# Attention scores of two token tiles at a time, with the lower-part products on half the rows of the array

## The chip, the core and the metric

The kernel runs on one core of a Trainium2 chip. The metric is the device time of one execution, in microseconds (us). The engines that matter here are PE (TensorE, the matrix engine; its weight loads are listed apart as PEld), DVE (VectorE), ACT (ScalarE), POOL (GpSimd) and SP, which issues most of the DMAs.

## The reference

The kernel computes one decoder layer for 1024 tokens of width 1024. Two token mixers run side by side: an attention with three branches (compressed blocks, selected blocks, a sliding window of 512) and an attention over a latent with an index that selects 256 keys for each query. Both have 8 heads. Their outputs are projected, gated, merged and normalized, and a mixture of 32 experts with a second normalization follows. The change touches only the logits of the attention:

```python
logits = jnp.einsum('tghd,gtkd->ghtk', q, k_g) * scale + bias          # selected blocks
logits = jnp.einsum('tghd,kgd->ghtk', q, kw) * scale + rel_a[...]       # window
logits = jnp.einsum('tghd,cgd->ghtc', q, k_cmp) * scale + rel_a[...]    # compressed blocks
logits = jnp.einsum('thr,tkr->htk', q_lat, c_g) * HEAD_DIM ** -0.5 + bias  # latent
```

A head has 64 values per query and key.

## The kernel before

All matrix products are made from numbers that are split into a higher part and a lower part (`split`, lines 58 to 60: ACT copies the higher part in the fp32r type, DVE subtracts it). For the scores a head's queries lie in one tile `q` of 128 partitions: `load_query` (L475 to L479) puts the higher part of the 64 values on partitions 0 to 63 and the lower part on partitions 64 to 127, with two DMAs of 256 KB, issued by SP. The keys' higher part lies in `kh` and the lower part in `kl`; each is held twice, on both halves of the partitions. One matmul of `q` with `kh` therefore gives (higher + lower query) times higher key, and one of `q` with `kl` adds the same with the lower key, into the same PSUM tile.

The tokens are cut into 8 tiles `i` of 128. `nsa_head` (L548) makes a head of the first mixer: for each half `gq` (four token tiles) and each `part` (0: selected blocks, 1: window and compressed blocks) it goes over the four tiles. A tile's score row has 128 x (i + 1) columns in part 0, at most 640 in part 1, and is cut into chunks of 512 columns. Every chunk is one matmul with `kh` (L573) and one with `kl` (L574). In part 1 a product of 64 columns with the compressed keys follows (L580 with `kch`, L581 with `kcl`). `dsa_head` (L631) does the same for the second mixer (L651 with `kh`, L652 with `kl`), and for tiles from 2 on a third matmul adds the selection as a mask (L654). Each score row has a PSUM tile `s` of two banks, and there are two of these (`ps.open("psa", s=2, pt=3, pv=1)`).

`softmax_part` (L481) then adds the bias on DVE (L482) and takes the exponential on ACT (L484); POOL scales the rows (L465). `values` (L523) transposes the probabilities on PE (L490, into the PSUM tiles `pt`), splits them (L59, L60), and multiplies them with the values (L545 and L546, into `pv`). Heads of the two mixers alternate (`ORDER`). The order of the instructions of each engine is made by a scheduler at build time that simulates the engines: it keeps the program's order as a priority and fills gaps with what is ready, so scores of one head stand between transposes and value products of another.

The only matmuls before that don't use all 128 rows of the array are those of `bias_tables` (L293, L294): nine pairs on 33 rows, between full-row matmuls of the projections (L204) and of the compressed blocks (L393).

Of the kernel before, what the change touches and what calls it, by code (L numbers as in the profile page):

```python
# [9 lines left out]
F32 = mybir.dt.float32  # L10
# [8 lines left out]
P = 128  # L19
T = 1024  # L20
# [24 lines left out]
def layer_kernel(ctx: ExitStack, tc: tile.TileContext, A, out, dbg=None):  # L45
    nc = tc.nc
    V, S, G, PE = nc.vector, nc.scalar, nc.gpsimd, nc.tensor
# [7 lines left out]
    def f(ap):  # L55
        return ap.bitcast(F32)
# [10 lines left out]
    class Psum:  # L67
# [7 lines left out]
        def tile(self, shape, dt, name):  # L75
            return self.pool.tile(shape, dt, name=name, bufs=self.bufs[name])

    ps = Psum()
# [3 lines left out]
    qkd = {n: (dr.tile([P, T], F32, name=f"h_{n}"), dr.tile([P, T], F32, name=f"l_{n}"))  # L82
           for n in TILES[3:15] if n not in ("kc", "vc")}
# [18 lines left out]
    ident_b = cst.tile([P, P], BF, name="ident_b")  # L102
# [10 lines left out]
    kch = att.tile([P, 2, 64], F32R, name="kch")  # L113
    kcl = att.tile([P, 2, 64], F32R, name="kcl")
# [6 lines left out]
    OFF = {}  # L121
# [5 lines left out]
    selm = att.tile([P, NIDX], BF, name="selm")  # L127
# [9 lines left out]
    with tc.tile_pool(name="cr", bufs=1, side="right") as cr, tc.tile_pool(name="cr2", bufs=2, side="right") as cr2:  # L137
        big = [ps.tile([P, T], F32, name="s") for _ in range(3)]
        acc = [b[:, c] for b in big for c in HALF] + [ps.tile([P, 512], F32, name=n) for n in ("pt", "pv")]
        for k in range(KD):  # L140
# [7 lines left out]
            for i in range(NT):  # L148
                ts = slice(i * P, (i + 1) * P)
# [78 lines left out]
    with tc.tile_pool(name="ix", bufs=1, side="right") as ix, tc.tile_pool(name="ixl", bufs=2, side="right") as ixl:  # L228
        qs = []
        for n in ("qi0", "qi1"):  # L230
            z = project(n)
            for j in range(2):
                t = ix.tile([P, T], F32R, name=f"qs{len(qs)}")
                a, b = slice(j * 64, j * 64 + 64), slice(64 - j * 64, 128 - j * 64)
# [7 lines left out]
        for g in range(2):  # L242
            t = ps.tile([P, 512], F32, name="pt")
# [180 lines left out]
    with tc.tile_pool(name="cp", bufs=1, side="right") as cp, tc.tile_pool(name="bt", bufs=1, side="right") as bt:  # L424
        bias = bias_tables(bt)
        for n in ("kc", "vc"):
            j = TILES.index(n)
            compress_in(n, cp)
            c = compress(n, cp)
# [28 lines left out]
    pwp = pws.enter_context(tc.tile_pool(name="pwp", bufs=1))  # L458
# [3 lines left out]
    aw1 = aw.enter_context(tc.tile_pool(name="aw1", bufs=3, side="right"))  # L462
# [10 lines left out]
        return t[:, 0], t[:, 1]  # L473

    def load_query(t, n, j):  # L475
        r = slice(j * 64, j * 64 + 64)
        for x in range(2):
            nc.sync.dma_start(f(t[x * 64:x * 64 + 64]), qkd[n][x][r])
        return t  # L479

    def softmax_part(s, m, p, st, j):  # L481
        V.tensor_tensor_reduce(p, s, m, scale=1.0, scalar=3.0e38, op0=ALU.add, op1=ALU.min,  # L482
                               accum_out=st[:, 0, j:j + 1])
        S.activation(p, p, AF.Exp, bias=st[:, 0, j:j + 1], scale=-1.0, accum_out=st[:, 1, j:j + 1])  # L484
# [16 lines left out]
    mc = aw0.tile([P, 8, 120], F32, name="mc")  # L501
# [47 lines left out]
    def nsa_head(h, kv, fin):  # L549
        g = h // 4  # L550
        ksh, ksl, kwh, kwl = kv
        if h % 2 == 0:
            pair["q"], pair["m"], pair["w"] = slot(2, [P, 2, T], F32R), slot(3, [P, 2, T]), slot(4, [P, 2, T])
        q, m, mw = (pair[x][:, h % 2] for x in "qmw")
        load_query(q, f"qa{h // 2}", h % 2)
        nc.sync.dma_start(m, toeplitz(b_d[h], WD, T))
        nc.sync.dma_start(mw[:, 0:640], toeplitz(bw_d[h], WW, 640))
        for gq in range(2):
            o = ps.tile([P, 512], F32, name="pv")
            I4 = range(4 * gq, 4 * gq + 4)  # L560
            todo = []
            for part in range(2):
                st = aw1.tile([P, 2, 8], F32, name="st", bufs=3)
                PR, PC, PS = {}, {}, {}
                for i in I4:
                    ts = slice(i * P, (i + 1) * P)
                    k0 = 0 if part == 0 else max(0, i - 4)
                    n = P * (i + 1 - k0)
                    kh, kl = (ksh, ksl) if part == 0 else (kwh, kwl)
                    s = ps.tile([P, T], F32, name="s")  # L570
                    for c in range(0, n, 512):
                        e = min(n, c + 512)
                        PE.matmul(s[:, c:e], q[:, ts], kh[:, k0 * P + c:k0 * P + e], start=True, stop=False)  # L573
                        PE.matmul(s[:, c:e], q[:, ts], kl[:, k0 * P + c:k0 * P + e], start=False, stop=True)  # L574
                    j = i % 4
                    if part == 0:
                        PR[i] = aw1.tile([P, T], F32, name="pb", bufs=8)[:, :n]
                        softmax_part(s[:, :n], m[:, T - n:T], PR[i], st, j)
                    else:
                        PE.matmul(s[:, 640:704], q[:, ts], kch[:, g], start=True, stop=False)  # L580
                        PE.matmul(s[:, 640:704], q[:, ts], kcl[:, g], start=False, stop=True)  # L581
                        pb = pwp.tile([P, 704], F32, name="pw", bufs=6)
                        PR[i], PC[i], PS[i] = pb[:, :n], pb[:, n:n + 64], pb[:, n - 64:n + 64]
                        softmax_part(s[:, :n], mw[:, 640 - n:640], PR[i], st, j)
                        softmax_part(s[:, 640:704], mc[:, h, 56 - 8 * i:120 - 8 * i], PC[i], st, 4 + j)
                w = 4 + 4 * part
                V.tensor_scalar(st[:, 1, :w], st[:, 1, :w], 1e-30, None, op0=ALU.max)
                V.reciprocal(st[:, 1, :w], st[:, 1, :w])
                V.tensor_tensor(st[:, 1, 0:4], st[:, 1, 0:4], sig[:, 4 * gq:4 * gq + 4, 3 * h + 1 + part], op=ALU.mult)
                if part:  # L590
                    V.tensor_tensor(st[:, 1, 4:8], st[:, 1, 4:8], sig[:, 4 * gq:4 * gq + 4, 3 * h], op=ALU.mult)
                for i in I4:
                    scale_rows(PR[i], st[:, 1, i % 4:i % 4 + 1])
                    if part:
                        scale_rows(PC[i], st[:, 1, 4 + i % 4:5 + i % 4])
                for k in range(4 * gq + 4):
                    ii = [i for i in I4 if i >= k and (part == 0 or i - 4 <= k)]
                    k0 = [0 if part == 0 else max(0, i - 4) for i in range(NT)]
                    todo.append((vv[:, k, 2 * part + g],
                                 [PR[i][:, (k - k0[i]) * P:(k - k0[i] + 1) * P] for i in ii], ii[0]))  # L600
                if part:
                    todo.append((vcc[:, g], [PS[i] for i in I4], 4 * gq))
                values(o, todo, gq, part == 0, part == 1)
                todo = []
            finish("a", h, gq, o, fin)
# [24 lines left out]
    def dsa_head(h, vb, fin):  # L630
        m = aw2.tile([P, T], F32, name="m")  # L631
        nc.sync.dma_start(m, toeplitz(b_d[8 + h], WD, T))
        q = load_query(aw2.tile([P, T], F32R, name="q"), f"qb{h // 2}", h % 2)
        s = ps.tile([P, T], F32, name="s")
        for w, c in ((ukh, cth), (ukh, ctl), (ukl, cth)):
            for x in HALF:
                PE.matmul(s[:, x], w[:, h], c[:, x], start=(w is ukh and c is cth), stop=(w is ukl))
        kh = aw2.tile([P, T], F32R, name="kbh", bufs=1)
        kl = aw2.tile([P, T], F32R, name="kbl", bufs=1)
        split(kh, kl, s)  # L640
        for gq in range(2):
            I4 = range(4 * gq, 4 * gq + 4)
            PR = {}
            st = aw1.tile([P, 2, 4], F32, name="st", bufs=3)
            for i in I4:
                ts = slice(i * P, (i + 1) * P)
                n = P * (i + 1)
                s = ps.tile([P, T], F32, name="s")
                for c in range(0, n, 512):
                    e = min(n, c + 512)  # L650
                    PE.matmul(s[:, c:e], q[:, ts], kh[:, c:e], start=True, stop=False)  # L651
                    PE.matmul(s[:, c:e], q[:, ts], kl[:, c:e], start=False, stop=i < 2)  # L652
                    if i >= 2:
                        PE.matmul(s[:, c:e], ident_b, selm[:, OFF[i] + c:OFF[i] + e], start=False, stop=True)  # L654
                PR[i] = aw1.tile([P, T], F32, name="pb", bufs=8)[:, :n]
                softmax_part(s[:, :n], m[:, T - n:T], PR[i], st, i % 4)
            V.tensor_scalar(st[:, 1], st[:, 1], 1e-30, None, op0=ALU.max)
            V.reciprocal(st[:, 1], st[:, 1])
            for i in I4:
                x = st[:, 1, i % 4:i % 4 + 1]  # L660
                if (i % 2 and h >= 6):
                    V.tensor_scalar(PR[i], PR[i], x, None, op0=ALU.mult)
                else:
                    scale_rows(PR[i], x)
            o = ps.tile([P, 512], F32, name="pv")
            todo = []
            for k in range(4 * gq + 4):
                ii = [i for i in I4 if i >= k]
                todo.append((vb[:, k, h % 2], [PR[i][:, k * P:(k + 1) * P] for i in ii], ii[0]))
            values(o, todo, gq, True, True)  # L670
            finish("b", h, gq, o, fin)
# [148 lines left out]
    with tc.tile_pool(name="wo", bufs=1, side="right") as wo, tc.tile_pool(name="wo2", bufs=2, side="right") as wo2:  # L820
# [147 lines left out]
        for i in range(NT):  # L968
            ts = slice(i * P, (i + 1) * P)
            s = ps.tile([P, T], F32, name="s")  # L970
            last = i == NT - 1
# [343 lines left out]
```

## Time and profile before

| | us |
|---|---|
| median of three runs | 1434.45 (1433.2 to 1434.85) |
| the profiled execution | 1431.84 |
| its span, first to last instruction | 1430.1 |
| PE busy | 1331.9 (93%) |
| DVE busy | 1114.9 (78%) |
| ACT busy | 764.4 (53%) |
| POOL busy | 460.3 (32%) |

The attention, which the change touches, lies between 435 and 835 us. A matmul's busy time in the profile holds its way through the array too, and matmuls overlap, so the pace of the PE is read from the distance between starts and not from durations.

### The profile page before, as it was taken

What the parts mean: (1) busy time and instruction counts of PE and PEld (TensorE: products, weight loads), DVE (VectorE), ACT (ScalarE), POOL (GpSimd) and SP (SyncE); (2) the same over time, 40 slices, a digit from 0 to 9 for tenths busy, and PEclk for the clock granted to TensorE, in tenths of its full rate; (3) what the DMA queues carried; (4) which work ended last, traced back from release to release, by engine and by line L of the source; (5) the groups of instructions that cost most, each with busy time, mean ns of one, the idle gap of its engine ahead of it and who ended that gap; (6) DMA issues with size and microseconds to landing.
All of it is one profiled execution on the core that took longest, in us unless ns stands there. A gap on an engine that the chain in (4) does not pass through costs nothing. (4 is left out here: it accounts for less than half of the span.)

```text
span 1430.1 us, 20066 instructions
## 1 busy us (share of the span) xinstructions
PE 1331.9 (93%) x6779; PEld 1100.2 (77%) x6795; DVE 1114.9 (78%) x2273; ACT 764.4 (53%) x1378; POOL 460.3 (32%) x463
## 2 busy tenths in 40 slices
PE   8999999999999999999999999999969999998960
PEld 7878888878887787888878778888757778776640
DVE  5323699889997787888889965655869999998856
ACT  4323323221116788888879731211238888886744
POOL 1112323222223335453444100001334454443326
PEclk9999999999998999999999999999969999999985
DMA  6023334498333232732521264664659999999936
GB/s 234 16 74 133 111 116 149 152 279 285 138 106 112 67 107 90 195 105 82 152 74 38 97 264 160 253 237 154 230 186 329 344 325 317 317 329 329 320 74 235
DMA packets 69477, 261.36 MB, mean 183 GB/s; under 512 B 15092, under 2 KB 16974, under 8 KB 57085
## 3 DMA queue, kind: packets, MB, share of 16 engines
q1 hardware_dynamic: 59644, 243.24, 49.3%
q0 software_dynamic: 9728, 16.82, 5.1%
q8 instruction: 54, 0.88, 0.3%
q14 instruction: 51, 0.41, 0.1%
HBM read 219.19 MB, written 70.70 MB: 203 GB/s over the span
## 5 line engine op out<-in xcount | busy, mean ns | idle before, releaser
L1089 PE MATMUL pt<-slot,slot 128*128 128x512 f32 x768 | 199.9, 407 | 10.3 <-DVE slot L1077 4.9
L1077 DVE TENSOR_TENSOR slot<-slot,slot 128x1024 fp32r<-128x1024 f32 x160 | 191.3, 1219 | 15.8 <-ACT slot L1076 11.7
L1076 ACT CAST slot<-slot 128x1024 fp32r<-128x1024 f32 x160 | 165.8, 1048 | 36.9 <-PE pt L1089 25.9
L1089 PEld LDWEIGHTS pt<-slot,slot 128*128 128x128 f32 x768 | 142.1, 192 | 49.7 <-DVE slot L1077 8.9
L186 POOL TENSOR_TENSOR wl<-wr,wh 128x1024 fp32r<-128x1024 f32 x39 | 94.9, 2434 | 264.5 <-ACT wh L185 256.0
L324 DVE TENSOR_SCALAR_CACHE_REDUCE jk<-idx,cand 128x384 bf16<-128x384 f32 (+1 forms) x186 | 164.4, 942 | 1.2
L60 DVE TENSOR_TENSOR ptl<-pt,pth 128x512 fp32r<-128x512 f32 (+1 forms) x240 | 148.5, 638 | 18.5 <-ACT pth L59 17.5
L204 PE MATMUL s<-xh,wh 128*128 128x512 f32 x496 | 154.9, 393 | 2.4 <-DVE wi L168 1.4
L204 PE MATMUL s<-xh,wl 128*128 128x512 f32 x496 | 154.5, 391 | 0.0
L204 PE MATMUL s<-xl,wh 128*128 128x512 f32 x496 | 154.4, 391 | 0.0
L59 ACT CAST pth<-pt 128x512 fp32r<-128x512 f32 (+1 forms) x240 | 127.8, 548 | 45.4 <-PE pt L490 38.6
L465 POOL TENSOR_SCALAR pb<-pb,st 128x128 f32<-128x128 f32 (+3 forms) x120 | 91.7, 783 | 183.1 <-ACT pth L59 55.5
L185 ACT CAST wh<-wr 128x1024 fp32r<-128x1024 f32 x39 | 41.0, 1051 | 190.9 <-PE s L204 92.2
L1117 POOL DMA_INDIRECT acc_d<-wr,tkv x32 | 76.8, 2400 | 138.7 <-DVE wr L1116 132.5
L204 PEld LDWEIGHTS s<-xh,wh 128*128 128x128 f32 x496 | 92.5, 188 | 22.9 <-issue 2.6
L204 PEld LDWEIGHTS s<-xl,wh 128*128 128x128 f32 x496 | 93.6, 189 | 19.5
L204 PEld LDWEIGHTS s<-xh,wl 128*128 128x128 f32 x496 | 93.4, 189 | 19.3
L484 ACT ACTIVATE pb<-pb,st 128x128 f32<-128x128 f32 (+7 forms) x128 | 99.6, 779 | 15.5 <-DVE st L482 14.4
L1112 PE MATMUL s<-slot,hT 128*128 128x512 f32 x384 | 100.7, 408 | 2.0 <-DVE hT L60 1.5
L982 PE MATMUL s<-slot,slot 128*128 128x512 f32 x384 | 93.5, 398 | 0.0
L1112 PEld LDWEIGHTS s<-slot,hT 128*128 128x128 f32 x384 | 70.6, 191 | 26.8 <-DVE hT L60 11.2
L490 PE MATMUL pt<-ident,pb 128*128 128x128 f32 x576 | 90.5, 276 | 0.7 <-DVE ptl L60 0.4
(340 smaller groups left out, 2918.8 us busy)
## 6 DMA issues: line engine op xcount, KB each, us to landing
slot<-in_w_ex_dram SPq DMA_DIRECT2D x80, 1024.0 KB
wr<-in_w_tt_dram SPq DMA_DIRECT2D x31, 512.0 KB
ring<-in_w_ex_dram SPq DMA_DIRECT2D x11, 1024.0 KB
b_d<-r_d SPq DMA_DIRECT2D x16, 576.0 KB
xw<-in_xw_dram SPq DMA_DIRECT2D x8, 718.0 KB
last<-in_w_ex_dram SPq DMA_DIRECT2D x5, 1024.0 KB
z_ga<-sh SPq DMA_DIRECT2D x8, 512.0 KB
slot<-b_d SPq DMA_DIRECT2D x8, 512.0 KB
```

Of the source, the lines that this page charges most:

```text
L59: S.copy(h, src)
L60: V.tensor_tensor(l, src, f(h), op=ALU.subtract)
L186: G.tensor_tensor(wl, wr, f(wh), op=ALU.subtract)
L204: PE.matmul(z[:, c], w[:, k * P:(k + 1) * P], xx[:, k, c], start=(k == 0 and w is wh and xx is xh), stop=(k == KD - 1 and w is wl))
L324: V.tensor_scalar(jk[:, :n], idx[:, OFF[i]:OFF[i] + n], t, None, op0=op, op1=ALU.add, accum_out=cnt[:, i - 2:i - 1])
L465: G.tensor_scalar(ap, ap, s, 1.0, op0=ALU.mult, op1=ALU.mult)
L484: S.activation(p, p, AF.Exp, bias=st[:, 0, j:j + 1], scale=-1.0, accum_out=st[:, 1, j:j + 1])
L982: mm = PE.matmul(s[:, HALF[c]], MS[i][:, a, k], WO[k][:, b, HALF[c]], start=(k == 0 and x == 0), stop=(k == KD - 1 and x == 2)).ins
L1076: S.copy(w[:, 0], self.w[k2 // 4][:, k2 % 4 // 2])
L1077: d = V.tensor_tensor(w[:, 1], self.w[k2 // 4][:, k2 % 4 // 2], f(w[:, 0]), op=ALU.subtract).ins
L1089: PE.matmul(self.a, self.xt[:, a, k * P:(k + 1) * P], w[:, b, (k - k2) * 512:(k - k2 + 1) * 512], start=(k == 0 and x == 0), stop=(k == KD ...
L1112: PE.matmul(s[:, c], self.hT[:, a, k * P:(k + 1) * P], w[:, b, c], start=(k == 0 and x == 0), stop=(k == 1 and x == 2))
```

## The change

`load_query` keeps the old stacking for even token tiles and turns it round for odd ones (the lower part on partitions 0 to 63, the higher part on 64 to 127). It issues four DMAs for a head instead of two, each of half the size with pieces of 128 tokens. A new helper `scores` takes two token tiles at a time. For each chunk it issues the full-row products with `kh` of both tiles, then the products with `kl`, each on 64 rows only: rows 0 to 63 for the even tile and 64 to 127 for the odd one. These rows hold the query's higher part, so the product of the two lower parts is no longer formed. The products with `kl` are tied behind the last one with `kh` of the chunk. In `dsa_head` the masks of both tiles follow. Both `s` tiles are taken before the first matmul of a pair, and `softmax_part` of both comes after the last.

```diff
     def load_query(t, n, j):
         r = slice(j * 64, j * 64 + 64)
         for x in range(2):
-            nc.sync.dma_start(f(t[x * 64:x * 64 + 64]), qkd[n][x][r])
+            for y in range(2):
+                nc.sync.dma_start(f(t[y * 64:y * 64 + 64]).rearrange("p (a b t) -> p a b t", b=2, t=P)[:, :, x ^ y],
+                                  qkd[n][x][r].rearrange("p (a b t) -> p a b t", b=2, t=P)[:, :, x ^ y])
         return t
+
+    def scores(q, kh, kl, jobs, last=True):
+        for c in range(0, max(n for _, _, _, n in jobs), 512):
+            for k in (kh, kl):
+                for s, i, k0, n in jobs:
+                    if c < n:
+                        e = min(n, c + 512)
+                        r = slice(0, P) if k is kh else slice(i % 2 * 64, i % 2 * 64 + 64)
+                        with tc.issue_after(d) if k is kl else nullcontext():
+                            m = PE.matmul(s[:, c:e], q[r, i * P:(i + 1) * P], k[r, k0 * P + c:k0 * P + e],
+                                          start=k is kh, stop=k is kl and (last or i < 2))
+                if k is kh:
+                    d = m.ins
+            if not last:
+                for s, i, k0, n in jobs:
+                    if c < n and i >= 2:
+                        e = min(n, c + 512)
+                        PE.matmul(s[:, c:e], ident_b, selm[:, OFF[i] + c:OFF[i] + e], start=False, stop=True)
@@ nsa_head
-                for i in I4:
...
-                    s = ps.tile([P, T], F32, name="s")
-                    for c in range(0, n, 512):
-                        e = min(n, c + 512)
-                        PE.matmul(s[:, c:e], q[:, ts], kh[:, k0 * P + c:k0 * P + e], start=True, stop=False)
-                        PE.matmul(s[:, c:e], q[:, ts], kl[:, k0 * P + c:k0 * P + e], start=False, stop=True)
...
+                for i2 in (4 * gq, 4 * gq + 2):
+                    jobs = []
+                    for i in (i2, i2 + 1):
+                        k0 = 0 if part == 0 else max(0, i - 4)
+                        jobs.append((ps.tile([P, T], F32, name="s"), i, k0, P * (i + 1 - k0)))
+                    scores(q, kh, kl, jobs)
+                    if part:
+                        scores(q, kch[:, g], kcl[:, g], [(s[:, 640:704], i, 0, 64) for s, i, _, _ in jobs])
+                    for s, i, k0, n in jobs:
...
@@ dsa_head
-            for i in I4:
...
+            for i2 in (4 * gq, 4 * gq + 2):
+                jobs = [(ps.tile([P, T], F32, name="s"), i, 0, P * (i + 1)) for i in (i2, i2 + 1)]
+                scores(q, kh, kl, jobs, last=False)
+                for s, i, _, n in jobs:
+                    PR[i] = aw1.tile([P, T], F32, name="pb", bufs=8)[:, :n]
+                    softmax_part(s[:, :n], m[:, T - n:T], PR[i], st, i % 4)
```

## Rows read from the trace of the kernel before

**Rows 1.** The page: busy time of each engine, and the granted clock in slices.

```profile
PE 1331.9 (93%) x6779; PEld 1100.2 (77%) x6795; DVE 1114.9 (78%) x2273; ACT 764.4 (53%) x1378; POOL 460.3 (32%) x463
...
PEclk9999999999998999999999999999969999999985
```

**Rows 2.** Attention, 435 to 835: length, busy PE, PEld, DVE, ACT, POOL, clock, DMA.

```profile
435.00:835.00 400.00, 386.00 (x2438) 327.57 (x2453) 338.40 (x940) 323.60 (x807) 165.00 (x253) 0.99 0.37 109
```

**Rows 3.** Waits of PE in 435 to 835: us in total, times, longest.

```profile
PE s L573 <- DVE st L482: 3.0, 7, 1.0
PE pv L546 <- DVE ptl L60: 2.5, 4, 1.0
```

**Rows 4.** Lines L574, L652, L581: weight loads, durations in ns, first and last start.

```profile
L574 PEld LDWEIGHTS s<-slot,slot x192: 187/189/333, 438.1 to 771.5; 128*128 128x128 f32 x192
...
L652 PEld LDWEIGHTS s<-kbl,q x96: 186/190/194, 469.4 to 815.8; 128*128 128x128 f32 x96
...
L581 PEld LDWEIGHTS s<-kcl,slot x64: 187/192/333, 440.6 to 771.7; 128*128 128x128 f32 x64
```

**Rows 5.** Timeline of PE around 33-row matmuls, 255.5 to 258.5.

```profile
255.67 0.62 PE L204 MATMUL s<-xl,wh 128*128 128x512 f32 x2
256.13 0.61 PE L204 MATMUL s<-xh,wl 128*128 128x512 f32 x2
256.67 0.40 PE L293 MATMUL s<-oh,relh 33*8 33x512 f32 x1
256.91 0.40 PE L294 MATMUL s<-oh,rell 33*8 33x512 f32 x1
257.24 0.49 PE L393 MATMUL pv<-wh,ch 128*128 128x256 f32 x1
257.56 0.38 PE L393 MATMUL pv<-wl,ch 128*128 128x256 f32 x1
257.79 0.63 PE L204 MATMUL s<-xh,wh 128*128 128x512 f32 x2
```

**Rows 6.** Timeline of all engines: start us, us, engine, line, operation.

```profile
503.71 0.24 PE L580 MATMUL s<-kch,slot 128*128 128x64 f32 x1
...
503.79 0.28 PE L581 MATMUL s<-kcl,slot 128*128 128x64 f32 x1
```

**Rows 7.** Timeline of PE around another such pair, 217.2 to 219.7.

```profile
217.49 0.38 PE L393 MATMUL pv<-wl,ch 128*128 128x256 f32 x1
217.72 0.38 PE L393 MATMUL pv<-wh,cl 128*128 128x256 f32 x1
218.03 0.39 PE L293 MATMUL s<-oh,relh 33*8 33x512 f32 x1
218.26 0.39 PE L294 MATMUL s<-oh,rell 33*8 33x512 f32 x1
218.58 0.73 PE L204 MATMUL s<-xh,wh 128*128 128x512 f32 x2
219.16 0.62 PE L204 MATMUL s<-xl,wh 128*128 128x512 f32 x2
```

**Rows 8.** Timeline of PEld, 255.5 to 258.5, idle time before in brackets.

```profile
256.67 0.08 PEld L293 LDWEIGHTS s<-oh,relh 33*8 33x8 f32 x1 [0.35 <-DVE jk L324]
...
257.23 0.29 PEld L393 LDWEIGHTS pv<-wh,ch 128*128 128x128 f32 x1 [0.47 <-issue]
```

**Rows 9.** Timeline of PE in the attention, a value product after transposes.

```profile
470.58 0.60 PE L490 MATMUL pt<-ident,pb 128*128 128x128 f32 x4
470.94 0.48 PE L546 MATMUL pv<-ptl,vv 128*128 128x512 f32 x1
471.25 0.40 PE L545 MATMUL pv<-pth,vv 128*128 128x512 f32 x1
```

**Rows 10.** Timeline of all engines: a query's load, and the matmul that waits for it.

```profile
508.85 0.59 SPq L478 DMA_DIRECT2D slot<-l_qa  x1
...
512.98 0.30 PE L573 MATMUL s<-slot,slot 128*128 128x128 f32 x1 [1.46 <-DMA slot<-l_qa]
```

More of the change, by code (lines that the diff above doesn't have):

```diff
@@ L564, in nsa_head @@
                 PR, PC, PS = {}, {}, {}
-                for i in I4:
[L566 to L569, printed above, removed]
-                    s = ps.tile([P, T], F32, name="s")
-                    for c in range(0, n, 512):
-                        e = min(n, c + 512)
-                        PE.matmul(s[:, c:e], q[:, ts], kh[:, k0 * P + c:k0 * P + e], start=True, stop=False)
-                        PE.matmul(s[:, c:e], q[:, ts], kl[:, k0 * P + c:k0 * P + e], start=False, stop=True)
[L575 to L585, printed above, removed]
@@ new lines, in nsa_head @@
+                kh, kl = (ksh, ksl) if part == 0 else (kwh, kwl)
+                for i2 in (4 * gq, 4 * gq + 2):
[7 more added lines that the diff above has]
+                    for s, i, k0, n in jobs:
+                        j = i % 4
+                        if part == 0:
+                            PR[i] = aw1.tile([P, T], F32, name="pb", bufs=8)[:, :n]
+                            softmax_part(s[:, :n], m[:, T - n:T], PR[i], st, j)
+                        else:
+                            pb = pwp.tile([P, 704], F32, name="pw", bufs=6)
+                            PR[i], PC[i], PS[i] = pb[:, :n], pb[:, n:n + 64], pb[:, n - 64:n + 64]
+                            softmax_part(s[:, :n], mw[:, 640 - n:640], PR[i], st, j)
+                            softmax_part(s[:, 640:704], mc[:, h, 56 - 8 * i:120 - 8 * i], PC[i], st, 4 + j)
@@ L644, in dsa_head @@
             st = aw1.tile([P, 2, 4], F32, name="st", bufs=3)
-            for i in I4:
[L646 to L656, printed above, removed]
+            for i2 in (4 * gq, 4 * gq + 2):
+                jobs = [(ps.tile([P, T], F32, name="s"), i, 0, P * (i + 1)) for i in (i2, i2 + 1)]
+                scores(q, kh, kl, jobs, last=False)
+                for s, i, _, n in jobs:
+                    PR[i] = aw1.tile([P, T], F32, name="pb", bufs=8)[:, :n]
+                    softmax_part(s[:, :n], m[:, T - n:T], PR[i], st, i % 4)
             V.tensor_scalar(st[:, 1], st[:, 1], 1e-30, None, op0=ALU.max)
```

## Prediction

> **What bounds the kernel now.** I read the page first: PE is busy for 93% of the span, DVE for 78%, and the granted clock stays in the top tenth in nearly every slice, so the array runs at 2.4 GHz where the change lies [rows 1]. Then the table of stretches: in the 400 us of the attention PE is busy for 386.0 us, DVE for 338.4, ACT for 323.6 [rows 2]. Busy PE time holds pipeline time, so I looked at its waits as well: the two largest in that stretch are 3.0 us (7 times, for the bias addition that frees a score tile) and 2.5 us [rows 3]. The PE is the bound, with DVE 48 us behind it. What the change adds to or takes from the PE's queue should move the end nearly one for one; a gain would be shared with DVE once it came near 48 us.
>
> **How many matmuls the change touches.** The lower-part products have 192, 96 and 64 weight loads in the three lines [rows 4]: 352 matmuls, hence 176 pairs (6 chunk pairs for a head's selected part, 6 for its window, 4 for its compressed keys, 6 for a latent head; 8 heads each).
>
> **What it removes.** On full rows, two matmuls of 512 columns start 0.46 us after the two before them (255.67, 256.13) [rows 5], so 0.23 us each, or 0.445 ns a column. If the two of a pair run beside each other on their halves of the array, a pair lasts as long as its longer member, and the shorter, always the even tile, costs nothing. The even tiles have 128+384+640+896 = 2048 columns in a full causal head (16 of these) and 128+384+640+640 = 1792 in a window (8): 47,104 columns, 21 us. The 64-column products start 0.08 us apart [rows 6]; 32 of them saved are 2.5 us. Together 23.5 us. No row of before shows two matmuls side by side, so the bounds are 0 (they follow one another as before) and 23.5. I take the upper end: the 33-row matmuls also start 0.23 to 0.24 us apart for 512 columns [rows 5, 7], so time goes by columns and not by rows, and half of the array is free for the other tile. The Trainium skill (TensorE: Matmul & The Clock Gate, "Part 3: Packing small matmuls") has such tiles start 4 ns apart, and no run so far shows that; by it the saving would be 23.5 us less 176 x 4 ns, the same within a microsecond.
>
> **What it adds: changes of the array's shape.** Each of the 176 pairs stands between full-row matmuls, so the PE goes from 128 rows to 64 and back 176 times. The nearest thing in the trace are the 33-row products of the bias tables. Around them I compare the starts with the normal pace. From 256.13, two matmuls of 512 columns, two on 33 rows of 512 and two of 256 columns (0.22 us each at their usual pace [rows 7]) should bring the next L204 to 256.13 + 0.46 + 0.46 + 0.44 = 257.49; it starts at 257.79 [rows 5], 0.30 us late. From 217.72 the sum is 0.22 + 0.46 + 0.46, so 218.86; the start is 219.16 [rows 7], again 0.30 late. Where it goes can be seen: the first 33-row matmul starts 0.31 us after one that needs 0.22 (0.09 lost), the first full one 0.32 to 0.33 after one that needs 0.23 (another 0.09), and the full one after that 0.10 later than its pace. Before both changes the weight load, otherwise started ahead of time, stands still for 0.35 and 0.47 us and begins only with its matmul [rows 8]. So the queue is emptied at each change, and the weights are not loaded ahead across it.
>
> The 33-row loads have 8 columns of weights; the new ones have 128. In the attention a 128-column load that is not made ahead costs 0.08 us (a value product after transposes: the next start is 0.31 us behind instead of 0.23) [rows 9], and I add that at the entry: 0.38. The second tile's load adds between nothing (it goes beside the first) and another 0.08; I take the middle, 0.04. One excursion costs 0.42 us, with bounds of 0.30 and 0.46. Below 0.30 only if 64 rows with all 128 columns are entered more cheaply than 33 rows with 8 columns; that is the first rival. 176 x 0.42 = 74 us, bounds 53 and 81.
>
> The Trainium skill has a rule against this change (TensorEngine Tiling (Array Packing), "Key Properties"): changing the tiling mode, not just the tile, drains the TensorE. It gives no figure, and the 0.30 us above are what the trace makes of it; without that rule's effect the sum would end 74 us lower.
>
> **What it adds: DMAs.** 16 heads load queries, each with two DMAs more: 32 more issues of 0.45 to 0.59 us on SP's queue [rows 10], 17 us on a queue that mostly waits. What stands behind them are bias rows and outputs of other heads, loaded a head ahead. Only where a new pair of heads begins in the first mixer does PE wait: once, 1.46 us, for the lower part of the query [rows 10]. Two more issues before it push that by about 1 us. I take 1 us; bounds 0 and 6 (four such starts, 1.5 us each).
>
> **What it moves.** A pair takes both score tiles at once, so PE cannot begin the next pair's second product before DVE has read both tiles. There are 96 pairs of tiles (4 in each of 24 score passes). Transposes and value products of other heads lie ready to fill in, a third to a half of PE's work there; and a slower PE gives DVE time, which shrinks the waits it causes now. I set the two against each other at 0; bounds -5 (the two waits of [rows 3]) and +41 (each of the 96 brings one wait of 3.0/7 = 0.43 us). The masks of both tiles now follow one another; same count, 0.
>
> **The sum.** 74 - 23.5 + 1 = +51.5 us. Against the profiled execution: 1431.84 + 51.5 = 1483. The median lies 2.6 us above that execution, so I predict 1486. With the bounds of the excursion (53 and 81) and the others at their middle, 1465 to 1493; with overlap, buffers and DMAs at their worse ends it goes past 1515. Its own range is 1462 to 1510.
>
> **Rivals.**
>
> *The change of shape is cheap (faster).* The 33-row products differ in two ways from the new ones: rows and, with 8 or 16 weight columns, columns too. If only the change of columns empties the array, the pairs slip in at pace. Then 23.5 us come off PE, DVE (338 busy) still fits beneath, and the time is 1411 to 1424, depending on how much DVE and ACT take back; I say 1416. The turning point is 23.5/176 = 0.13 us an excursion. Against it: both changes, in and out, cost the same 0.09 us, and the weight load stood still before both. For it: no row shows a change of rows alone. The Trainium skill (TensorE: Matmul & The Clock Gate, "Part 3: Packing small matmuls") has weight loads for other row groups pulled ahead of running matmuls, which is this rival's mechanism. By that rule the loads before the 33-row matmuls need not have stood still; there they did [rows 8].
>
> *The pairs don't overlap (slower).* The change then does not do what it says: 352 matmuls at the old pace and 176 excursions of 0.38: 67 + 1 = +68, so 1502. For it: no row shows two matmuls side by side; against it: separate rows and separate PSUM banks.
>
> *The pair starves the PE (slower still).* The 96 waits of 0.43 us come on top of the forecast: +41, 1527; or on top of the cheap case: 1457. Against it: the scheduler has other heads' work, and PE waits little for DVE now [rows 3].
>
> *A balance.* An excursion costs between 0.10 and 0.15 us: within 0.2% of 1434.
>
> **Chances.** Forecast 0.56, no overlap 0.10, starving 0.06, cheap change 0.22, balance 0.06. That makes slower 0.72, same 0.06, faster 0.22, with 0.2% as about what a measurement of this kernel tells from no change. The range has to reach into the cheap case: 1416 to 1515 leaves out its lower half (0.11) and the top of the two slow rivals (0.07).
>
> **What the profile after would show.** If the step on shape is right, every pair of lower-part products is preceded by an idle weight-load queue, its first start lies about 0.3 us behind the full product of 512 columns before it, and the full product after it is late by 0.1; the stretch of the attention grows from 400 to about 450 us with the same busy DVE time. If the overlap is right, the two starts of a pair are less than 0.1 us apart. If the starving rival is right, PE's waits for the bias addition rise from 3 us to tens. What would make the prediction wrong is a pair that starts 0.23 us after its predecessor with its weights loaded ahead: then the attention shrinks by about 20 us.

## The result: 61 us slower, and the profile after

| | us |
|---|---|
| before, median of four (the three of above and one more) | 1433.83 |
| changed, median of four | 1494.47 (1491.92 to 1495.54) |
| ratio | 1.0419, 95% interval 1.0405 to 1.0433 |
| profiled execution of the changed kernel | 1494.55, its span 1492.6 |

A ratio is estimated from all executions, so it can differ by up to 0.2% from the quotient of two medians.

The page's first part, and the granted clock in slices, of the changed kernel (before: [rows 1]):

```profile
PE 1380.2 (92%) x6779; PEld 1094.8 (73%) x6795; DVE 1118.3 (75%) x2273; ACT 765.0 (51%) x1378; POOL 455.3 (31%) x463
...
PEclk9999999999988899999999999999969999999995
```

DVE, ACT and POOL are busy as long as before; PE has 48 us more, and in three slices of the attention the clock is below its upper level, where it was so in one. The attention alone, from 435 us to the last transpose, as in [rows 2]: length, then busy PE, PEld, DVE, ACT, POOL, then the clock.

```profile
435.00:897.00 462.00, 433.96 (x2439) 322.73 (x2454) 341.35 (x939) 324.24 (x807) 160.42 (x253) 0.95 0.32 94
```

The kernel before, cut at its own last transpose:

```profile
435.00:834.50 399.50, 385.65 (x2437) 327.46 (x2452) 338.28 (x939) 323.10 (x806) 165.00 (x253) 0.99 0.37 109
```

The attention takes 462.0 us instead of 399.5, which is the whole difference of the two spans (62.5 us). PE is idle for 28.0 us of it (13.8 before), and its largest wait has grown from the 3.0 us in 7 times of [rows 3] (us in total, times, longest):

```profile
PE s L493 <- DVE st L504: 11.0, 25, 1.4
```

A pair in its place, timeline of PE in the changed kernel (L493 is every score product, L501 the mask), and below it the weight loads:

```profile
576.23 0.39 PE L493 MATMUL s<-kbh,q 128*128 128x512 f32 x1
576.54 0.49 PE L493 MATMUL s<-kbl,q 64*128 64x512 f32 x2
576.97 0.60 PE L501 MATMUL s<-selm,ident_b 128*128 128x512 bf16 x2
577.23 0.58 PE L493 MATMUL s<-kbh,q 128*128 128x128 f32 x2
577.73 0.39 PE L493 MATMUL s<-kbl,q 64*128 64x128 f32 x2
```

```profile
576.54 0.19 PEld L493 LDWEIGHTS s<-kbl,q 64*128 64x128 f32 x2 [0.30 <-issue]
576.97 0.11 PEld L501 LDWEIGHTS <-ident_b 128*128 128x128 bf16 x2 [0.24 <-issue]
```

Both products of the pair lie within 0.49 us, and both their weight loads within 0.19. A single product of this shape takes as long where it stands alone (from the experiment with one tile at a time below):

```profile
600.29 0.50 PE L658 MATMUL s<-kbl,q 64*128 64x512 f32 x1
```

So the two run side by side. But the first starts 0.31 us after a full product that needs 0.23, the masks start 0.43 us after a pair that needs 0.23, and the weight loads stood still for 0.30 and 0.24 us before. This is what [rows 5, 7, 8] showed around the 33-row products.

### The profile page after: what moved, and what is told of

The parts are those of the page before. It is cut to its first block, busy times and chain, and to the rows that moved or that the text cites. A ratio compares the mean times of both kernels' runs of the same rounds, so it can differ in the third digit from the quotient of the medians.

```text
span 1492.6 us, 20139 instructions
## 1 busy us (share of the span) xinstructions
PE 1380.2 (92%) x6779; PEld 1094.8 (73%) x6795; DVE 1118.3 (75%) x2273; ACT 765.0 (51%) x1378; POOL 455.3 (31%) x463
## 5 line engine op out<-in xcount | busy, mean ns | idle before, releaser
L1091 DVE TENSOR_TENSOR slot<-slot,slot 128x1024 fp32r<-128x1024 f32 x160 | 191.4, 1220 | 17.1 <-ACT slot L1090 13.0
L493 PE MATMUL s<-slot,slot 64*128 64x512 f32 (+7 forms) x384 | 107.6, 432 | 13.5 <-DVE st L504 11.0
L512 PE MATMUL pt<-ident,pb 128*128 128x128 f32 x576 | 98.0, 288 | 3.7 <-POOL pb L465 2.5
L493 PEld LDWEIGHTS s<-slot,slot 64*128 64x128 f32 (+1 forms) x384 | 54.4, 197 | 55.6 <-issue 30.3
```

Source lines behind the costliest of these rows:

```text
L493: m = PE.matmul(s[:, c:e], q[r, i * P:(i + 1) * P], k[r, k0 * P + c:k0 * P + e], start=k is kh, stop=k is kl and (last or i < 2))
L512: PE.transpose(t[:rows, x * P:(x + 1) * P], c, ident)
L1091: d = V.tensor_tensor(w[:, 1], self.w[k2 // 4][:, k2 % 4 // 2], f(w[:, 0]), op=ALU.subtract).ins
```

## The experiments

A visit is one stay of the PE on 64 rows. All kernels but the two with small matmuls differ from the kernel before in the attention alone. The medians stand beside the kernel before of the same chip; between runs of different chips, the distances from that kernel are compared.

### Pairs on all 128 rows

```diff
-                        r = slice(0, P) if k is kh else slice(i % 2 * 64, i % 2 * 64 + 64)
+                        r = slice(0, P)
```

> The changed kernel, but the lower-part products use all 128 rows again; two tiles at a time, both score tiles taken at once and the four query loads stay. Theory (each visit to 64 rows costs about 0.37 us, 176 visits, less the overlap; the rest is a lower clock that these visits bring): without visits the time goes back to 1434 to 1441 us and the granted clock in the attention to 0.98 or more. Rival (taking both score tiles at once starves the PE): it stays above 1455.

Measured: 1464.84 against 1431.93 us, ratio 1.0235 (1.0217 to 1.0253). The theory fell here, and the rival's range (above 1455) holds: without a single visit, more than half of the loss stays. The theory's clock, 0.98 or more, is there, but the time is not. The attention takes 433.4 us, and PE is idle for 33.3 of it:

```profile
435.00:868.40 433.40, 400.08 (x2436) 332.54 (x2451) 342.83 (x938) 323.69 (x807) 161.41 (x253) 0.98 0.34 101
```

Waits of PE (for DVE, and for the rows that POOL scales) and of DVE in this kernel:

```profile
PE s L493 <- DVE st L504: 11.8, 25, 2.2
...
PE pt L512 <- POOL pb L465: 3.3, 6, 1.2
...
PE pt L512 <- POOL pw L465: 1.8, 2, 1.0
...
DVE pw L504 <- PE s L493: 18.1, 20, 2.0
```

PE and DVE wait for each other. The wait for a free score tile has grown by 8.8 us from the 3.0 of [rows 3], and waits for POOL of 5.1 us are new; these two are most of the 19.5 us by which PE's idle time grew. The timeline of this kernel shows how:

```profile
578.52 1.07 PE L493 MATMUL s<-slot,slot 128*128 128x384 f32 x4
579.43 0.30 PE L493 MATMUL s<-kch,slot 128*128 128x64 f32 x2
579.57 0.39 PE L493 MATMUL s<-kcl,slot 128*128 128x64 f32 x2
...
579.88 0.56 DVE L504 CUSTOM_DVE_ANT_0 pw<-s,slot 128x384 f32<-128x384 f32 x1 [1.64 <-PE s L493]
```

Eight products of two tiles stand in a row, and DVE, idle for 1.64 us, gets the first score row only when nearly all of them are done. With both score tiles full at the same moment, PE then has none free to go on with.

### The same pairs, tile after tile

```diff
-            for k in (kh, kl):
-                for s, i, k0, n in jobs:
+        for s, i, k0, n in jobs:
+            for c in range(0, n, 512):
                 (full product, lower product, mask of this tile and chunk, all on 128 rows;
                  the tie of the lower products goes with the old order)
```

> The paired kernel on 128 rows, but within a pair all products of the first tile (full, lower part, mask) stand before those of the second; both score tiles are still taken ahead and both softmax parts still stand behind. Theory (the order of the products starves the PE: no row of the pair is ready before three quarters of its products, and the next pair's first row not before both tiles are read): back to 1430 to 1440 us. Rival (taking both tiles and both softmax parts together is what costs): as the paired kernel on 128 rows, 1460 to 1467.

Measured: 1435.40 against 1433.18 us, ratio 1.0009 (0.9995 to 1.0022). The loss is gone, though both tiles are taken ahead and both softmax parts still stand behind. The waits are those of [rows 3] again:

```profile
PE s L490 <- DVE st L496: 3.0, 7, 1.0
```

So it is the order of the products within a pair, with the tie that holds it, that costs 33 us, and nothing else of the pairing. The overlap needs the two lower-part products next to each other, and the changed kernel gets that by this order. Another order wasn't tried: both lower-part products first, and then the full products tile after tile, which would finish the first tile earlier and still keep the pair together.

### The query loads alone

```diff
@@ load_query of the kernel before
-            nc.sync.dma_start(f(t[x * 64:x * 64 + 64]), qkd[n][x][r])
+            (the four loads of the changed kernel)
```

> The kernel before with the four query loads of the changed kernel alone (odd tiles stacked the other way, all products on 128 rows). Theory: 0 to 1 us more, 1433 to 1436. Rival (smaller pieces and more issues delay the start of the heads): 6 us more or above, 1440.

Measured: 1432.45 against 1431.93 us, ratio 1.0012 (0.9999 to 1.0024): half a microsecond, not to be told from none.

### Both tiles on the same 64 rows

```diff
-                        r = slice(0, P) if k is kh else slice(i % 2 * 64, i % 2 * 64 + 64)
+                        r = slice(0, P) if k is kh else slice(0, 64)
```

(with the query loads of the kernel before)

> The changed kernel, but both tiles of a pair use rows 0 to 63 for the lower-part product (queries stacked as before, two loads a head): the same 176 visits, no two products side by side. Theory (the pairs overlap fully in the changed kernel): 21 to 24 us slower than the changed kernel, 1515 to 1518. Rival (they don't overlap): the same as the changed kernel, 1492 to 1497.

Measured: 1527.96 against 1433.75 us, ratio 1.0663 (1.0621 to 1.0706). That is some 33 us slower than the changed kernel, 10 us more than the overlap is worth by its columns and above both ranges. By the table below, 23.4 us of it are the overlap and 12 the lower clock, with 3.5 us less idle time.

### One tile at a time on 64 rows

```diff
@@ the kernel before, with the changed query loads
-                        PE.matmul(s[:, c:e], q[:, ts], kl[:, ...], start=False, stop=True)
+                        x = slice(i % 2 * 64, i % 2 * 64 + 64)
+                        PE.matmul(s[:, c:e], q[x, ts], kl[x, ...], start=False, stop=True)
```

> The kernel before in its own order, one tile at a time, with the queries stacked as in the changed kernel and every lower-part product on 64 rows: 352 visits to 64 rows, nothing side by side. Theory (0.26 to 0.29 us a visit at full clock, as the runs so far give it): 92 to 102 us more, 1525 to 1536, and above that only by what a lower clock adds. Rival (0.42 us a visit, as predicted): 148 us more, 1582.

Measured: 1568.71 against 1433.18 us, ratio 1.0924 (1.0882 to 1.0966). Its four executions lie far apart (1560.8 to 1576.9, with a granted clock from 0.944 to 0.931), and the profiled one is the slowest of them. The attention:

```profile
435.00:978.50 543.50, 538.23 (x2443) 384.26 (x2457) 346.43 (x940) 332.15 (x807) 164.48 (x253) 0.88 0.27 80
```

PE is idle for 5.3 us only, and the clock is at 0.88. By time alone a visit costs 135.5/352 = 0.38 us, nearer to the rival (0.42); with the lower clock set apart it is 0.26, see the table.

### Fewer visits

```diff
+        for s, i, k0, c, e in parts:      # all full products of both tiles
+            d = PE.matmul(s[:, c:e], q[...], kh[...], start=True, stop=False).ins
+        for s, i, k0, c, e in parts:      # then all lower-part products
+            r = slice(0, P) if full else slice(i % 2 * 64, i % 2 * 64 + 64)
...
+                        scores(q, kch[:, g], kcl[:, g], [...], full=True)
```

> The changed kernel with fewer visits to 64 rows: all full products of a pair of tiles first, then all its lower-part products, and the compressed keys' lower parts on 128 rows: 96 visits instead of 176. Theory: 96 x 0.37 = 35.5, less 21 for the overlap: 14.5 us more than before, and up to 15 for a lower clock: 1448 to 1464. Rival (the pair's two score tiles starve the PE, visits don't matter): no better than 1490.

Measured: 1465.89 against 1431.93 us, ratio 1.0242 (1.0223 to 1.0261). It just misses the expected range, and the rival (no better than 1490) misses by more. The time is that of the pairs on 128 rows and 1 us more. By the table, the 96 visits less their overlap add 4.7 us of work and the lower clock 1.7, and the idle time is 3.8 us less, 2.6 us together in the profiled executions.

```diff
@@ the changed kernel, compressed keys alone
+                        r = slice(0, P) if k is kh or full else slice(...)
```

> The changed kernel with the compressed keys' lower parts on 128 rows: 32 visits fewer (144), and 32 products of 64 columns no longer overlapped. Theory: 32 x 0.37 - 2.5 = 9 us faster than the changed kernel, 1483 to 1488. Rival (visits are free, starving costs): as the changed kernel or 2 us slower, 1494 to 1497.

Measured: 1483.74 against 1431.93 us, ratio 1.0377 (1.0354 to 1.0400), 10.7 us less than the changed kernel (8.8 by the distances from the kernel before). The number is as expected, the reason is not: by the table, the gain lies in the clock. There the 32 visits saved, less the overlap given up, come to 0.8 us of work, or (0.8 + 2.5)/32 = 0.10 us a visit; why these cost less than the others is not shown.

### The price of a visit by itself

```diff
@@ project(), the kernel before
+            if k < KD - 1:
+                PE.matmul(z[:, 0:16], wh[0:64, k * P:(k + 1) * P], zero[0:64], start=False, stop=False)
```

> The kernel before, with one small matmul added after each of the first seven steps of each of the 31 projections: 64 rows, 128 columns of weights, 16 moving columns of zeros that are added to the result: 217 visits to 64 rows in a stretch where PE never waits. Theory: 0.36 us each, 78 us more, 1505 to 1520. Rival (only a change of columns empties the array): as the same matmul on 128 rows, 13 to 17 us more, 1447 to 1451.

> As the kernel with 217 small matmuls on 64 rows, but on 128 rows: 0.06 to 0.08 us each by the pace of small products in the attention. Both theories: 13 to 17 us more than before, 1447 to 1451.

Measured: 1529.20 us with 64 rows and 1466.84 with 128, both against 1433.75 (ratios 1.0659, 1.0623 to 1.0696, and 1.0224, 1.0187 to 1.0262). Both lie above their ranges: each small matmul costs more than expected on 128 rows too (33/217 = 0.15 us). The difference of the two is the change of shape alone: 62.4/217 = 0.29 us. It is there with all 128 columns, so the rival that only a change of columns empties the array falls. The timeline of PE, first on 64 rows, then on 128:

```profile
150.43 0.62 PE L206 MATMUL s<-xh,wl 128*128 128x512 f32 x2
150.97 0.27 PE L209 MATMUL s<-zero,wh 64*128 64x16 f32 x1
151.18 0.73 PE L206 MATMUL s<-xh,wh 128*128 128x512 f32 x2
151.75 0.62 PE L206 MATMUL s<-xl,wh 128*128 128x512 f32 x2
```

```profile
151.47 0.63 PE L206 MATMUL s<-xh,wl 128*128 128x512 f32 x2
151.93 0.17 PE L209 MATMUL s<-zero,wh 128*128 128x16 f32 x1
151.96 0.71 PE L206 MATMUL s<-xh,wh 128*128 128x512 f32 x2
152.50 0.62 PE L206 MATMUL s<-xl,wh 128*128 128x512 f32 x2
```

From the first line to the last are 1.32 us with the visit and 1.03 without, for the same four full products and one small one. The four take 0.92 us at their pace, so the small matmul adds 0.40 us on 64 rows and 0.11 on 128; 0.29 is what the half rows add.

### Only the long pairs

```diff
+        if full or jobs[0][1] < 4:
+            for job in jobs:
+                tile_scores(q, kh, kl, [job], True, last)
+        else:
+            tile_scores(q, kh, kl, jobs, False, last)
```

> Only the pairs of token tiles 4 to 7, whose rows are longest, use 64 rows, each pair in one visit for all its chunks; the other tiles and the compressed keys keep 128 rows and the order of the kernel before. 48 visits at 0.26 us are 12.5 us, the overlap saves 34,816 columns or 15.5 us. Theory (the order of a pair's products starves the PE whatever the visits cost): half of the pairs bring half of the 34 us of the paired kernel on 128 rows, 14 us net: 1444 to 1452. Rival (only the number of visits decides): 3 us faster than before, 1429 to 1432.

Measured: 1447.50 against 1433.72 us, ratio 1.0087 (1.0053 to 1.0121). Of the kernels here with products side by side it is the fastest, and it is still 14 us slower than before, where by visits and columns alone it should be 3 us faster. By the table nothing is lost in the work; idle time has grown by 10.4 us and the lower clock costs 8.4. That this is the order's share fits the theory, but these pairs were not run on 128 rows.

### All of them in one account

For each kernel, of its attention (435 us to the last transpose): its length, PE's idle time, the time for which the lower clock was granted (over stretches of 6 us, twice what the granted clock lacks of 1), and the rest, which is the length less the idle time less half of the time at the lower clock. The rest stands for the queue's own work at 2.4 GHz. Short waits that hide behind a modelled end of a matmul are in it too.

| kernel | visits | overlap | length | idle | lower clock | rest |
|---|---|---|---|---|---|---|
| before | 0 | | 399.5 | 13.8 | 10.2 | 380.6 |
| tile after tile | 0 | | 400.1 | 13.8 | 13.7 | 379.4 |
| pairs on 128 rows | 0 | | 433.4 | 33.3 | 20.5 | 389.8 |
| long pairs | 48 | 15.5 | 418.0 | 24.2 | 27.1 | 380.2 |
| fewer visits | 96 | 21 | 436.0 | 29.5 | 24.0 | 394.5 |
| compressed on 128 rows | 144 | 21 | 449.4 | 28.2 | 20.3 | 411.0 |
| changed | 176 | 23.5 | 462.0 | 28.0 | 44.4 | 411.8 |
| same 64 rows | 176 | 0 | 493.8 | 24.5 | 68.3 | 435.2 |
| one tile at a time | 352 | 0 | 543.5 | 5.3 | 129.6 | 473.4 |

A visit, by the rest: (473.4 - 380.6)/352 = 0.26 us in the order of before; (435.2 - 389.8)/176 = 0.26 in the order of the pairs; 0.29 where measured by itself. The overlap: 435.2 - 411.8 = 23.4 us. The order of the products: 9.2 us in the rest (what they are isn't shown) and 19.5 of idle time, and 5 us of clock. Set against the kernel before, the visits of the changed kernel come to (411.8 + 23.5 - 380.6)/176 = 0.31 us; that counts the 9.2 us as theirs. The changed kernel against before: 31.2 in the rest, 14.2 of idle time, 17.1 of clock, together 62.5.

Half of the time at the lower clock is an approximation. In the changed kernel at the lower level (timeline of PE, then of the weight loads):

```profile
508.94 0.63 PE L567 MATMUL pv<-pth,vb 128*128 128x512 f32 x1
509.37 1.06 PE L512 MATMUL pt<-ident,pb 128*128 128x128 f32 x4
```

```profile
506.39 0.29 PEld L493 LDWEIGHTS s<-slot,slot 64*128 64x128 f32 x2 [0.53 <-issue]
507.12 0.50 PEld L493 LDWEIGHTS s<-slot,slot 128*128 128x128 f32 x2 [0.44 <-issue]
```

A product of 512 columns holds the queue for 0.43 us instead of 0.23, a little less than twice. Leaving 64 rows (here after a pair of 512 columns) costs 0.73 - 0.43 = 0.30 us instead of 0.20, clearly less than twice. So the halving takes somewhat too much out, most of all from the kernel with one tile at a time, and its 0.26 is a low value.

## Why the prediction came out right

The time lies 8 us above the forecast of 1486 and inside its range, and the direction and its main reason hold. But that the sum comes so near is luck: the price of a visit was too high, the order of the products and the clock were left out, and these errors have opposite signs.

**The bound.** Right: PE sets the end, and what its queue gains or loses moves it. The length of the attention accounts for all of the difference.

**The counts and the overlap.** Right: 176 pairs, and 23.4 us measured where 23.5 stood. The Trainium skill (TensorE: Matmul & The Clock Gate, "Part 3: Packing small matmuls") has such tiles run side by side, and here the trace agrees: two products in 0.49 us, one alone in 0.50.

**The change of the array's shape.** The mechanism is right, the term too large: 0.42 us a visit was forecast, and by the account the mean is 0.26 to 0.31, or 46 to 55 us instead of 74. The 0.30 us from the 33-row products was already near. Of what I added, the 0.04 us for the second load is not there: both loads start at once. The 0.08 us for the longer load comes from a wrong reading of [rows 9]. A transpose alone takes 0.27 us in that trace, so four that take 0.60 start 0.11 us apart; 4 x 0.11 + 0.23 are the 0.67 us from 470.58 to 471.25, and nothing is lost there. A single visit differs with its place: in the chain with masks above, 0.08 us at its start and 0.20 at its end; around the small matmuls 0.40, where a small product on 128 rows costs 0.11. Why the mean lies at the lower end is not shown. The Trainium skill's rule (TensorEngine Tiling (Array Packing), "Key Properties") that a change of the tiling mode drains the TensorE agrees with all of these rows.

**What the pairs move.** This is the step that failed. I set it at 0 within bounds of -5 and +41, and gave the starving rival 0.06; measured by itself it is 33 us (1464.84 against 1431.93). The single wait was priced well: 0.43 us forecast, 11.8/25 = 0.47 and 11.0/25 = 0.44 measured. But it comes 25 times and not 96, and most of the loss is elsewhere: waits for POOL, work in the rest, the clock. So the sign that I had named, waits for the bias addition in the tens of us, stayed at 11. I named the right mechanism, that PE can't go on before DVE has read both tiles, and then let other heads' work cover it, from the share of such work and not from its place. PE's waits in [rows 3] are small because the first tile of two is complete while the second is made; the new order takes that away. The wait that I read as a sign that there was room was the product of the order that the change gives up.

**The clock.** Not in the sum at all. The lower clock was granted for 44.4 us of the attention instead of 10.2, 17 us of work, 5 of which come with the order alone. The kernel with compressed keys on 128 rows has the same rest and the same idle time as the changed one and 24 us less at the lower clock, and its attention is 12.6 us shorter, as half of 24 would have it. It also has 32 visits less, which by the mean price and less the overlap should have taken 5.8 us out of the rest; so this pair of runs doesn't set the clock's price apart from theirs.

**The DMAs.** 1 us forecast, 0.5 measured, within the uncertainty.

**The rivals.** Cheap shapes: refuted by the small matmuls, 0.29 us against a turning point of 0.13. No overlap: refuted by both tiles on the same rows. Starvation on top: true in kind, but it did not add fully; the changed kernel has 28.0 us of idle time, the pairs without visits 33.3, and that the visits' own time fills the difference is argued. A balance: its lower end, 0.10 us, gives 5 us less, which is 0.3% and not 0.2.

## What to carry to other kernels

Half-row products side by side do halve their time, but every visit to half rows, in and out, costs some 0.26 to 0.31 us here, more than a 512-column product; at 0.445 ns a column it pays only if it saves clearly more than 580 to 700 columns. Before interleaving two tiles' products to bring partners together, look at who reads them: with two buffers, finishing one tile early is what keeps the reader busy and the PE supplied. And test an enabling reorder alone, with the trick itself left out; here that one run held more than half of the loss.

## What the hardware showed that I had not expected

The granted clock falls to 1.2 GHz although PE looks fully busy. In the kernel with one tile at a time (length, busy PE, PEld, DVE, ACT, POOL, clock):

```profile
516.00:519.00 3.00, 3.00 (x13) 1.81 (x13) 2.07 (x9) 2.78 (x10) 1.18 (x2) 1.00 0.22 87
519.00:522.00 3.00, 3.00 (x8) 1.73 (x9) 1.36 (x4) 0.89 (x4) 0.00 (x0) 0.70 0.00 0
...
531.00:534.00 3.00, 3.00 (x11) 1.80 (x10) 1.62 (x6) 2.25 (x5) 0.00 (x0) 0.98 0.91 303
534.00:546.00 12.00, 12.00 (x38) 9.20 (x38) 3.80 (x15) 5.47 (x16) 3.78 (x4) 0.50 0.09 34
```

Before both falls PE is busy for 3.00 of 3 us, in a stretch full of visits (five of the 13 products of the first line); over the attention it is at the lower level for 129.6 us with 5.3 us idle. In the changed kernel such a stretch follows one with waits:

```profile
494.00:500.00 6.00, 5.06 (x26) 3.47 (x26) 3.15 (x14) 5.10 (x15) 3.06 (x4) 1.00 0.67 184
500.00:512.00 12.00, 12.00 (x41) 8.22 (x40) 5.57 (x27) 5.75 (x20) 5.92 (x13) 0.50 0.22 66
```

So the kernel with the most visits has the lower clock for longest although its PE is the least idle. Visits don't always bring it: the 217 small matmuls on 64 rows, each between dense full products, left the granted clock of the whole execution at 0.969, as on 128 rows. Which part of a visit makes the difference was not tried.
